# Two heads of a pair in one product at the inverse's second level, Silu on ScalarE, and decay tiles by head

## The chip, the cores and the metric

The kernel runs on one core of a Trainium2 chip, as one program. The metric is the device time of one execution in microseconds. Of three timed runs the median is 2611.71 us (2611.56 to 2614.45). TensorE is called PE in the profile (PEld are its weight loads), VectorE DVE, ScalarE ACT, GpSimd POOL, SyncE SP.

## The reference

A trunk of two layers over 512 tokens of width 1024. Each layer normalises x, projects it once into the inputs of three branches and three groups of gates, and adds the gated branches:

```python
for l in range(DEPTH):
    h = rmsnorm(x, norm_mix[l])
    (dq, dk, dv, dz, db, da, sq, sk, sv, iq, ik, iw, xq, gl) = jnp.split(h @ w_in[l], split_pts, axis=-1)
    o_dn = deltanet_branch(dq, dk, dv, dz, db, da, conv_w[l], a_log[l], dt_bias[l], dn_norm[l])
    o_sa = dsa_branch(sq, sk, sv, iq, ik, iw, positions)
    o_xa = memory_branch(xq, rmsnorm(mem, norm_mem[l]), w_mem_kv[l])
    ...
    x = x + merged @ w_out[l]
    h = rmsnorm(x, norm_ffn[l])
    gt, up = jnp.split(h @ w_ffn_in[l], 2, axis=-1)
    x = x + (jax.nn.silu(gt) * up) @ w_ffn_out[l]
return rmsnorm(x, norm_final)
```

The change is in the DeltaNet branch (8 heads of width 128, a causal convolution of 4 taps and Silu on q, k and v, a gated delta rule):

```python
qkv = jax.nn.silu(causal_conv(jnp.concatenate([q_in, k_in, v_in], axis=-1), conv_w))
q = l2norm(q) * DN_DK ** -0.5; k = l2norm(k)
...
decay = jnp.where(incl, jnp.exp(jnp.where(incl, diff, 0.0)), 0.0)
m = jnp.where(strict, jnp.einsum('bnhid,bnhjd->bnhij', kb, kc) * decay, 0.0)
sol = lax.linalg.triangular_solve(m, rhs, left_side=True, lower=True, unit_diagonal=True)
...
o = rmsnorm(o, dn_norm) * jax.nn.silu(z)
```

## The kernel before, in words

Everything is f32. A weight matrix comes as units of 128 x 1024: SP loads a unit into `wr` (three buffers), ACT rounds it to `wh` (L269, three buffers) and DVE takes the rest `wl` (L270, two buffers). A product with weights is three products of rounded parts, hi x hi, hi x lo, lo x hi (L277 to L279), 24 of them for a unit. Tiles of 128 x 512 come from one pool `P` of 43 slots; PSUM has three banks for weight products (`g`), two for small work (`a`), one `r` and two `o`.

The order of the work is made when the program is built. `Flow` holds a clock and a list of chains (generators). Each step of a weight product moves the clock on, and a chain whose time has come gets to write its next piece; `yield pe, lat` says how much PE time the piece took and how long its result needs. Then the framework's own scheduler puts each engine's instructions in an order, by dependencies and priority. On the chip each engine runs its own list in that order and waits on semaphores.

A layer runs: keys and values of the memory (`mem_kv`), the norm (`norm_chain`, with the sum over partitions at L300 and the spread at L308), the small gates (`misc`), index scores, cross attention, then the DeltaNet stage: four pairs of heads, each with `dn_qk` (k and q of both heads through `conv_silu2`), `dn_z` and `dn_v`, and a chain `dn_chain`. In layer 0 the top-k search runs on DVE beside it. After that come sparse attention, the output projection and the feed-forward (L1027 is its Silu).

`conv_silu2` (L528 to L538) copies the product to `x` and scales it into `y` on ACT, adds three shifted taps on DVE (L535), and takes Tanh of y/2 on ACT (L537); DVE then forms (tanh + 1) * y, which is twice Silu (L586 for k and q, L807 for v, L834 for z). The factor 2 is taken out later, in `hdn`, `hnk` and the small constants under the roots.

`decay_tiles` (L540) makes, for four heads, tiles of decays: one tile per chunk t, with the heads side by side. Each is a product with a mask, then Exp on ACT (L559). `dn_chain` transposes and squares k and q (L596, L603), forms k k^T and k q^T (L638) and multiplies them chunk by chunk with the decays (L641, L643, L647).

`inverse` solves the unit triangular blocks. M of 128 x 128 per chunk and head is cut into blocks of 32, whose inverses come from a forward substitution on DVE (L692, L694) over data that SP carries through DRAM (`dm`, `du`). Level one joins blocks of 32 to 64 (L715, L724). Level two joins 64 to 128: M times the upper inverse goes into `pa` (L734), its lower half is copied to `xz` (L735, L736), and a product with the lower inverse goes into `pb` (L741) and, negated, into `ub`. Each head a of a pair has its own `xt[a]`, `xz[a]` and four products per level; `xt` and `xz` hold zeros in the half that is not used.

Of the kernel before, what the change touches and what calls it, by code (L numbers as in the profile page):

```python
# [21 lines left out]
S = 512  # L22
# [94 lines left out]
def kernel(ctx: ExitStack, tc: tile.TileContext, A: dict, out: bass.AP):  # L117
# [171 lines left out]
    def rms_chain(tiles, n, tok, rs):  # L289
# [4 lines left out]
        for k in range(1, 8):  # L294
            q = ybuf()
            SC.activation(q[:, :n], tiles[k], AF.Square)
            V.tensor_add(acc[:, :n], acc[:, :n], q[:, :n])
            yield 0, 0.6
        for m in range(nt):
            PE.matmul(pt[:, m:m + 1], acc[:, m * 128:m * 128 + 128], ones[:, 0:1], start=m == 0, stop=True,  # L300
                      skip_group_check=True)
# [13 lines left out]
    def norm_chain(tiles, gain, act):  # L315
        rs = small([128, S], "nrs", 1)
        yield from rms_chain(tiles, S, small([128, 4], "ntok", 1), rs)
# [33 lines left out]
    def layer(l, xs, mact):  # L351
# [9 lines left out]
        norm = flow.spawn(norm_chain(xs, nmix[:, l], act))  # L361
# [166 lines left out]
    def conv_silu2(ps, l, idx):  # L528
        y, s = ybuf(), sbuf()
# [7 lines left out]
        SC.activation(s, y, AF.Tanh, scale=0.5)  # L537
        return y, s  # L538

    def decay_tiles(tk, grp):  # L540
        gsl = slice(4 * grp, 4 * grp + 4)
# [5 lines left out]
        def chain():  # L547
            for t in range(4):
                rd = []
                for nm in ("gh", "gl"):  # L550
                    r = sb.tile([128, 4, 128], F32R, name="rd" + nm, tag="rd" + nm, bufs=2)
                    V.tensor_mul(r, mb, tk[nm][:, t, gsl][:, :, None].to_broadcast([128, 4, 128]))
                    rd.append(r)
                yield 0, 2.0
                for w, dst in ((strict_r, dc4[t]), (ones_r, eg4[t])):
# [4 lines left out]
                V.tensor_mul(dc4[t], dc4[t], mb)  # L560
                V.tensor_copy(cd4[:, t], eg4[t][:, :, 127])
# [4 lines left out]
    def dn_qk(l, p, pairs, act, tk):  # L566
# [10 lines left out]
        for a in range(2):  # L577
            h = 2 * p + a
            kq.append([big(F32, (128, 2, 2, 128)) for _ in range(2)])
            for j, (kind, base) in enumerate((("dk", 8), ("dq", 0))):  # L580
                ps = gbank()
                gemm(ps, unit((kind, l, h)), act)
                y, s = conv_silu2(ps, l, base + h)
                for b in range(2):
                    bs = slice(256 * b, 256 * b + 256)
                    V.scalar_tensor_tensor(kq[a][b][:, :, j], s[:, bs].rearrange("p (t i) -> p t i", t=2), 1.0,  # L586
                                           y[:, bs].rearrange("p (t i) -> p t i", t=2),
                                           op0=ALU.add, op1=ALU.mult)
# [25 lines left out]
    def dn_chain(l, p, P, kq, tk):  # L614
# [8 lines left out]
        V.tensor_scalar(x, P.ss, 4.0 * EPS, None, op0=ALU.add)  # L623
        rsqrt_small(x, y, w)
        V.scalar_tensor_tensor(hnk, x, 0.5, y, op0=ALU.mult, op1=ALU.mult)
# [3 lines left out]
        V.tensor_scalar(P.sq, P.sq, 128.0 * EPS, 512.0 * EPS * EPS, op0=ALU.mult, op1=ALU.add)  # L629
        for a in range(2):  # L630
# [3 lines left out]
            for t2 in range(2):  # L634
# [4 lines left out]
                for tt in range(2):  # L639
                    t = 2 * t2 + tt  # L640
                    V.scalar_tensor_tensor(P.mt[a][:, t], pam[:, tt, 0], brk[:, a, t:t + 1], dc4[t][:, h4],  # L641
                                           op0=ALU.mult, op1=ALU.mult)
                    V.tensor_mul(P.at[a][:, t], pam[:, tt, 1], dc4[t][:, h4])  # L643
                yield 0.9, 0.5
            for t in range(4):
                qv = kq[a][t // 2][:, t % 2, 1]
                V.tensor_mul(qv, qv, eg4[t][:, h4])  # L647
# [24 lines left out]
    def inverse(l, p, P):  # L672
# [32 lines left out]
        yield 0, 8.0  # L705
# [3 lines left out]
        for a in range(2):  # L709
            for r in (0, 32):  # L710
                V.transpose(xt[a][r:r + 32, :, r:r + 32], ub[a][r:r + 32, :, r:r + 32])
            V.transpose(tt[64:96, a], ub[a][64:96, :, 64:96])
            for t in range(4):
# [7 lines left out]
        for a in range(2):  # L721
# [4 lines left out]
            for r in (0, 64):  # L726
                SC.activation(ub[a][r:r + 32, :, r + 32:r + 64], pu[r:r + 32, a], AF.Copy, scale=-1.0)
        for a in range(2):
            V.transpose(xt[a][32:64, :, 0:32], ub[a][0:32, :, 32:64])
        yield 1.0, 1.5  # L730
        pa = abank((128, 2, 4, 64))
        for a in range(2):
            for t in range(4):
                PE.matmul(pa[:, a, t], mt[a][:, t], xt[a][:, t], start=True, stop=True)  # L734
        SC.copy(xz[0][64:128, :, 0:64], pa[64:128, 0])  # L735
        V.tensor_copy(xz[1][64:128, :, 0:64], pa[64:128, 1])  # L736
        yield 1.8, 0.8
        pb = abank((128, 2, 4, 64))
        for a in range(2):
            for t in range(4):  # L740
# [513 lines left out]
```

## Time and profile before

| | |
|---|---|
| median of three runs | 2611.71 us |
| the profiled execution | 2612.87 us |
| its span, first to last instruction | 2611.1 us |
| PE busy | 2577.6 us (99%), 13336 matmuls |
| DVE busy | 1648.0 us (63%) |
| ACT busy | 1091.7 us (42%) |

The rows below come from one profiled execution, whose time is a little above the median. PE's busy share counts matmuls whose ends are modelled and overlap, so the cost of one is read from the start of it to the start of the next. Times in the timelines are in us from the start of the span. An f32 product counts as two instructions in the profile and as one in the order.

### The profile page before, as it was taken

Reading aid. Unit: us, or ns where it says so; the run is one execution under the profiler, and the core shown is the slowest. Engines: PE = TensorE matmul, PEld = TensorE weight load, DVE = VectorE, ACT = ScalarE, POOL = GpSimd, SP = SyncE. Lnnn points to the kernel's source line nnn. Section 1 sums busy time; section 2 is a strip of 40 time slices with the busy share of each in tenths; the row PEclk is TensorE's granted clock in tenths of the full one; section 3 lists DMA queues with packets and bytes.
Section 4 is the critical chain, followed back from the end, with each engine's and each line's share of the span. In section 5 each row is a group of like instructions: output and inputs, shape, how many; then the busy total and the mean of one; then the engine's idle time right before and its main releaser. Section 6 shows DMA issues by size and latency. Waiting matters only on the chain.

```text
span 2611.1 us, 35686 instructions
## 1 busy us (share of the span) xinstructions
PE 2577.6 (99%) x13336; PEld 2150.4 (82%) x13336; DVE 1648.0 (63%) x3701; ACT 1091.7 (42%) x2094; POOL 51.6 (2%) x124
## 2 busy tenths in 40 slices
PE   8999999999999999999999999999999999999997
PEld 7888887888888888888898888788888888888886
DVE  7895798764665554434478949887456645544344
ACT  5652545442454343323356426553425543333221
POOL 2000000000000000000000000000000000000000
PEclk9999999999999999999999999999999999999998
DMA  6213322224222332223352142222332123232222
GB/s 223 89 58 120 100 71 71 77 71 138 77 70 73 122 100 97 97 98 113 117 168 73 65 129 91 74 69 76 96 113 73 66 81 129 97 97 97 97 95 75
DMA packets 105724, 250.93 MB, mean 96 GB/s; under 512 B 37888, under 2 KB 38528, under 8 KB 105552
## 3 DMA queue, kind: packets, MB, share of 16 engines
q1 hardware_dynamic: 104656, 247.16, 29.2%
q8 instruction: 105, 1.72, 0.3%
q0 software_dynamic: 896, 1.51, 0.2%
q14 instruction: 67, 0.55, 0.1%
HBM read 236.98 MB, written 11.63 MB: 95 GB/s over the span
## 4 chain that ended last, share of the span: by engine, by line
PE 90%; DVE 7%; ACT 2%; issue 1%; DMA 1%; SPq 0%; DVEq 0%; ACTq 0%
PE g L277 26%; PE g L278 26%; PE g L279 26%; DVE y L535 2%; DVE wl L270 1%; PE o L277 1%; PE a L638 1%; PE a L279 1%; PE a L277 1%; PE a L278 1%; PE r L960 1%; PE o L278 1%; DVE utmp L692 1%; PE o L279 1%; DVE u L694 1%
## 5 line engine op out<-in xcount | busy, mean ns | idle before, releaser
L270 DVE TENSOR_TENSOR wl<-wr,wh 128x1024 fp32r<-128x1024 f32 (+1 forms) x418 | 506.3, 1211 | 570.1 <-PE g L279 397.0
L277 PE MATMUL g<-hh,wh 128*128 128x512 f32 (+1 forms) x2064 | 821.6, 398 | 0.0
L278 PE MATMUL g<-hl,wh 128*128 128x512 f32 (+1 forms) x2064 | 814.0, 395 | 0.0
L279 PE MATMUL g<-hh,wl 128*128 128x512 f32 (+1 forms) x2064 | 812.7, 394 | 0.0
L269 ACT CAST wh<-wr 128x1024 fp32r<-128x1024 f32 (+1 forms) x418 | 436.7, 1045 | 840.0 <-PE g L278 689.2
L279 PEld LDWEIGHTS g<-hh,wl 128*128 128x128 f32 (+1 forms) x2064 | 387.8, 188 | 77.0
L278 PEld LDWEIGHTS g<-hl,wh 128*128 128x128 f32 (+1 forms) x2064 | 388.7, 188 | 70.9 <-DVE hl L167 0.5
L277 PEld LDWEIGHTS g<-hh,wh 128*128 128x128 f32 (+1 forms) x2064 | 388.5, 188 | 70.7
L277 PE MATMUL g<-P,wh 128*128 128x512 f32 (+1 forms) x992 | 374.1, 377 | 7.4 <-ACT wh L269 7.4
L279 PE MATMUL g<-P,wl 128*128 128x512 f32 (+1 forms) x992 | 373.7, 377 | 0.5 <-DVE wl L270 0.5
L278 PE MATMUL g<-P,wh 128*128 128x512 f32 (+1 forms) x992 | 373.6, 377 | 0.0
L277 PEld LDWEIGHTS g<-P,wh 128*128 128x128 f32 x992 | 188.0, 190 | 41.2 <-ACT wh L269 7.5
L279 PEld LDWEIGHTS g<-P,wl 128*128 128x128 f32 x992 | 187.9, 189 | 34.6 <-DVE wl L270 0.8
L278 PEld LDWEIGHTS g<-P,wh 128*128 128x128 f32 x992 | 188.0, 190 | 33.5
L535 DVE SCALAR_TENSOR_TENSOR y<-x,k_conv_w,y 128x511 f32<-128x511 f32 x144 | 107.5, 746 | 7.9 <-ACT y L532 6.7
L167 DVE TENSOR_TENSOR P<-y,P 128x512 fp32r<-128x512 f32 (+1 forms) x86 | 59.4, 690 | 46.3 <-ACT P L166 46.3
L166 ACT CAST P<-y 128x512 fp32r<-128x512 f32 (+1 forms) x86 | 53.4, 620 | 83.1 <-DVE y L1031 43.8
L278 PE MATMUL g<-wl,hh 128*128 128x256 f32 x256 | 72.4, 283 | 0.0
L279 PE MATMUL g<-wh,hl 128*128 128x256 f32 x256 | 72.4, 283 | 0.0
L277 PE MATMUL g<-wh,hh 128*128 128x256 f32 x256 | 72.4, 283 | 0.0
L166 ACT CAST P<-r 128x256 fp32r<-128x256 f32 (+2 forms) x96 | 39.0, 406 | 64.1 <-PE r L960 45.4
L537 ACT ACTIVATE s<-y 128x512 f32<-128x512 f32 x48 | 30.3, 632 | 81.1 <-DVE y L535 70.0
(295 smaller groups left out, 3179.6 us busy)
## 6 DMA issues: line engine op xcount, KB each, us to landing
wr<-wu SPq DMA_DIRECT2D x400, 512.0 KB, 3.5
wr<-wf SPq DMA_DIRECT2D x16, 384.0 KB, 3.1
P<-xT SPq DMA_DIRECT2D x16, 256.0 KB, 5.1
park<-P SPq DMA_DIRECT2D x16, 256.0 KB, 4.1
P<-dm SPq DMA_DIRECT2D x64, 64.0 KB, 2.0
P<-park SPq DMA_DIRECT2D x16, 256.0 KB, 4.5
P<-memT SPq DMA_DIRECT2D x8, 256.0 KB, 4.6
d_x<-P SPq DMA_DIRECT2D x8, 256.0 KB, 4.1
```

Source lines behind the costliest of these rows:

```text
L166: SC.copy(hi, src)
L167: V.tensor_sub(lo, src, hi)
L269: SC.copy(wh[:, :cols], raw[:, :cols])
L270: V.tensor_sub(wl[:, :cols], raw[:, :cols], wh[:, :cols])
L277: PE.matmul(ps, lh, rh, start=start, stop=False, skip_group_check=skip)
L278: PE.matmul(ps, lh, rl, start=False, stop=False, skip_group_check=skip)
L279: PE.matmul(ps, ll, rh, start=False, stop=stop, skip_group_check=skip)
L535: V.scalar_tensor_tensor(y[:, sh:], x[:, :S - sh], cw[:, l, idx, j:j + 1], y[:, sh:], op0=ALU.mult, op1=ALU.add)
L537: SC.activation(s, y, AF.Tanh, scale=0.5)
L638: PE.matmul(pam[:, tt], kk[:, 0], kk, start=True, stop=True)
L692: V.tensor_mul(tv, u[:, :n, j:j + 1].to_broadcast([128, n, m]), mp[j // 16][:, j % 16:j % 16 + 1, j + 1:].to_broadcast([128, n, m]))
L694: V.tensor_sub(u[:, :n, j + 1:], u[:, :n, j + 1:], tv)
```

## The change

Level two of the inverse now treats both heads of a pair in one product. A new buffer `mz` takes the block of M that is needed, head 0's in rows 0 to 63 and columns 64 to 127, head 1's in rows 64 to 127 and columns 0 to 63, by two DMAs on SP's queue. Level one puts head 1's `xt` into the lower half of `xt[0]` with a copy on ACT, and head 1's lower inverse into the upper right of `ub[0]` with another, and `pa` and `pb` are four products each for the pair. Since `mz`, `xz` and `xt[0]` are shared, a list `packing` lets one pair at a time into this part; the waiting times in the yields change with it (8 to 7 and at least one more, 1.5 to 2.0, 1.8 to 0.9).

`conv` no longer takes Tanh; ACT applies Silu to y and writes k and q (two halves each) or v in place, and z straight from PSUM. The factors of 2 go: `4 * EPS` becomes `EPS`, the 0.5 in `hnk` and `hdn` falls away. Decay tiles are made per head with the four chunks side by side, so that DVE multiplies two chunks at once (L643 and L647 of before). The norm of layer 0 gets 4 units of waiting ahead of its sum over partitions.

```diff
...
-    def norm_chain(tiles, gain, act):
+    def norm_chain(tiles, gain, act, wait=0.0):
...
+        yield 0, wait
...
-        norm = flow.spawn(norm_chain(xs, nmix[:, l], act))
+        norm = flow.spawn(norm_chain(xs, nmix[:, l], act, 0.0 if l else 4.0))
...
-    def conv_silu2(ps, l, idx):
-        y, s = ybuf(), sbuf()
+    def conv(ps, l, idx):
+        y = ybuf()
...
-        SC.activation(s, y, AF.Tanh, scale=0.5)
-        return y, s
+        return y
...
-            for t in range(4):
+            for h in range(4):
                 rd = []
                 for nm in ("gh", "gl"):
                     r = sb.tile([128, 4, 128], F32R, name="rd" + nm, tag="rd" + nm, bufs=2)
-                    V.tensor_mul(r, mb, tk[nm][:, t, gsl][:, :, None].to_broadcast([128, 4, 128]))
+                    V.tensor_mul(r, mb, tk[nm][:, :, 4 * grp + h:4 * grp + h + 1].to_broadcast([128, 4, 128]))
                     rd.append(r)
                 yield 0, 2.0
-                for w, dst in ((strict_r, dc4[t]), (ones_r, eg4[t])):
+                for w, dst in ((strict_r, dc4[h]), (ones_r, eg4[h])):
                     pd = abank((128, 4, 128))
                     PE.matmul(pd, w, rd[0], start=True, stop=False)
                     PE.matmul(pd, w, rd[1], start=False, stop=True)
                     SC.activation(dst, pd, AF.Exp)
-                V.tensor_mul(dc4[t], dc4[t], mb)
-                V.tensor_copy(cd4[:, t], eg4[t][:, :, 127])
+                V.tensor_mul(dc4[h], dc4[h], mb)
+                V.tensor_copy(cd4[:, :, h], eg4[h][:, :, 127])
...
-                y, s = conv_silu2(ps, l, base + h)
+                y = conv(ps, l, base + h)
                 for b in range(2):
                     bs = slice(256 * b, 256 * b + 256)
-                    V.scalar_tensor_tensor(kq[a][b][:, :, j], s[:, bs].rearrange("p (t i) -> p t i", t=2), 1.0,
-                                           y[:, bs].rearrange("p (t i) -> p t i", t=2),
-                                           op0=ALU.add, op1=ALU.mult)
+                    SC.activation(kq[a][b][:, :, j], y[:, bs].rearrange("p (t i) -> p t i", t=2), AF.Silu)
...
-                for tt in range(2):
-                    t = 2 * t2 + tt
-                    V.scalar_tensor_tensor(P.mt[a][:, t], pam[:, tt, 0], brk[:, a, t:t + 1], dc4[t][:, h4],
+                for t in (2 * t2, 2 * t2 + 1):
+                    V.scalar_tensor_tensor(P.mt[a][:, t], pam[:, t % 2, 0], brk[:, a, t:t + 1], dc4[h4][:, t],
                                            op0=ALU.mult, op1=ALU.mult)
-                    V.tensor_mul(P.at[a][:, t], pam[:, tt, 1], dc4[t][:, h4])
+                ts = slice(2 * t2, 2 * t2 + 2)
+                V.tensor_mul(P.at[a][:, ts], pam[:, :, 1], dc4[h4][:, ts])
                 yield 0.9, 0.5
-            for t in range(4):
-                qv = kq[a][t // 2][:, t % 2, 1]
-                V.tensor_mul(qv, qv, eg4[t][:, h4])
+            for t2 in range(2):
+                qv = kq[a][t2][:, :, 1]
+                V.tensor_mul(qv, qv, eg4[h4][:, 2 * t2:2 * t2 + 2])
...
-        yield 0, 8.0
+        yield 0, 7.0
+        while packing:
+            yield 0, 1.0
+        packing.append(p)
+        SP.dma_start(mz[0:64, :, 64:128], mt[0][0:64, :, 64:128])
+        SP.dma_start(mz[64:128, :, 0:64], mt[1][0:64, :, 64:128])
+        yield 0, 1.0
...
+            if a:
+                SC.copy(xt[0][64:128], xt[1])
...
+        SC.copy(ub[0][0:64, :, 64:128], ub[1][64:128, :, 64:128])
         for a in range(2):
-            V.transpose(xt[a][32:64, :, 0:32], ub[a][0:32, :, 32:64])
-        yield 1.0, 1.5
-        pa = abank((128, 2, 4, 64))
-        for a in range(2):
-            for t in range(4):
-                PE.matmul(pa[:, a, t], mt[a][:, t], xt[a][:, t], start=True, stop=True)
-        SC.copy(xz[0][64:128, :, 0:64], pa[64:128, 0])
-        V.tensor_copy(xz[1][64:128, :, 0:64], pa[64:128, 1])
-        yield 1.8, 0.8
-        pb = abank((128, 2, 4, 64))
-        for a in range(2):
-            for t in range(4):
-                PE.matmul(pb[:, a, t], xz[a][:, t], ub[a][:, t, 64:128], start=True, stop=True)
-        SC.activation(ub[0][0:64, :, 64:128], pb[0:64, 0], AF.Copy, scale=-1.0)
-        V.tensor_scalar(ub[1][0:64, :, 64:128], pb[0:64, 1], -1.0, None, op0=ALU.mult)
-        yield 1.8, 0.8
+            V.transpose(xt[0][64 * a + 32:64 * a + 64, :, 0:32], ub[a][0:32, :, 32:64])
+        yield 1.0, 2.0
+        pa = abank((128, 4, 64))
+        for t in range(4):
+            PE.matmul(pa[:, t], mz[:, t], xt[0][:, t], start=True, stop=True)
+        SC.copy(xz[64:128, :, 0:64], pa[64:128])
+        V.tensor_copy(xz[0:64, :, 64:128], pa[0:64])
+        yield 0.9, 0.8
+        pb = abank((128, 4, 64))
+        for t in range(4):
+            PE.matmul(pb[:, t], xz[:, t], ub[0][:, t, 64:128], start=True, stop=True)
+        SC.activation(ub[0][0:64, :, 64:128], pb[0:64], AF.Copy, scale=-1.0)
+        V.tensor_scalar(ub[1][0:64, :, 64:128], pb[64:128], -1.0, None, op0=ALU.mult)
+        packing.clear()
+        yield 0.9, 0.8
...
-            y, s = conv_silu2(ps, l, 16 + h)
-            V.scalar_tensor_tensor(y, s, 1.0, y, op0=ALU.add, op1=ALU.mult)
+            y = conv(ps, l, 16 + h)
+            SC.activation(y, y, AF.Silu)
...
-            s = sbuf()
-            SC.activation(s, ps, AF.Tanh, scale=0.5)
             z = big()
-            V.scalar_tensor_tensor(z, s, 1.0, ps, op0=ALU.add, op1=ALU.mult)
+            SC.activation(z, ps, AF.Silu)
...
-    xt = [cst([128, 4, 64], name=f"xt{a}") for a in range(2)]
-    xz = [cst([128, 4, 128], name=f"xz{a}") for a in range(2)]
-    for t_ in xt + xz:
+    xt = [cst([128, 4, 64], name="xt0"), cst([64, 4, 64], name="xt1")]
+    xz, mz = (cst([128, 4, 128], name=n) for n in ("xz", "mz"))
+    packing = []
+    for t_ in xt + [xz, mz]:
...
```

Three places in the order show how instructions move. The first is PE in the second pair of layer 0, around level two: `xt_76` and `xt_77` are the two heads' tiles, `mz` the new buffer, `g` rows are weight products. Before:

```order
L278 MATMUL g<-hl,wh 128x512
L734 MATMUL a<-xt_76,P 128x64 x4
L734 MATMUL a<-xt_77,P 128x64 x4
L279 MATMUL g<-hh,wl 128x512
L277 MATMUL g<-hh,wh 128x512
L278 MATMUL g<-hl,wh 128x512
L741 MATMUL a<-P,xz_78 128x64 x4
L741 MATMUL a<-P,xz_79 128x64 x4
L596 MATMUL a<-k_ident,P 128x128 x4
```

And now:

```order
L278 MATMUL g<-hl,wh 128x512
L739 MATMUL a<-xt_76,mz 128x64 x4
L279 MATMUL g<-hh,wl 128x512
L277 MATMUL g<-hh,wh 128x512
L278 MATMUL g<-hl,wh 128x512
L279 MATMUL g<-hh,wl 128x512
L277 MATMUL g<-hh,wh 128x512
L745 MATMUL a<-P,xz 128x64 x4
L593 MATMUL a<-k_ident,P 128x128 x4
```

Eight products each have become four, and five weight products stand between them in place of three. Over the program PE has 12488 products before and 12424 now.

The second place is ACT at the first head of layer 0's DeltaNet stage, where convolution, activation and the decay tiles' Exp (L559, now L558) meet. Before:

```order
L269 CAST wh<-wr 128x1024
L531 COPY x<-g 128x512
L532 ACTIVATE y<-g,k_conv_w 128x512
L537 ACTIVATE s<-y 128x512
L559 ACTIVATE P<-a 128x512 x2
```

And now:

```order
L269 CAST wh<-wr 128x1024
L532 COPY x<-g 128x512
L533 ACTIVATE y<-g,k_conv_w 128x512
L585 ACT_TABLE_LOAD
L585 ACTIVATE P<-y 128x2x128 x2
L558 ACT_TABLE_LOAD
L558 ACTIVATE P<-a 128x512 x2
```

A table load stands ahead of Silu and another ahead of Exp. The program has 6 table loads before and 26 now. On PE the first transposes of k (L596, now L593) stand eleven weight products further back.

The third place is DVE at the start, around the norm's last square sums (L297) and the reading of L300's result (L303, now L304). Before:

```order
L297 TENSOR_TENSOR s<-s,y 128x512 x2
L270 TENSOR_TENSOR wl<-wr,wh 128x1024
L297 TENSOR_TENSOR s<-s,y 128x512
L847 TENSOR_TENSOR y<-g,mrs 128x512
L303 TENSOR_SCALAR rx<-a 128x4
L270 TENSOR_TENSOR wl<-wr,wh 128x1024
L608 TENSOR_SCALAR ntok<-rx 128x4
```

And now:

```order
L297 TENSOR_TENSOR s<-s,y 128x512 x2
L270 TENSOR_TENSOR wl<-wr,wh 128x1024
L297 TENSOR_TENSOR s<-s,y 128x512
L850 TENSOR_TENSOR y<-g,mrs 128x512
L270 TENSOR_TENSOR wl<-wr,wh 128x1024
L167 TENSOR_TENSOR P<-y,P 128x512
L304 TENSOR_SCALAR rx<-a 128x4
L605 TENSOR_SCALAR ntok<-rx 128x4
```

A weight's low half and another subtraction have moved ahead of the reading of the sum. On PE, L300 (now L301) stands eighteen weight products further back.

## Rows read from the trace of the kernel before

**Rows 1.** The page's head and its first two parts: the span, TensorE's busy time, share and instructions, and the clock that was granted in 40 slices (tenths of the full level).

```profile
span 2611.1 us, 35686 instructions
...
PE 2577.6 (99%) x13336; PEld 2150.4 (82%) x13336; DVE 1648.0 (63%) x3701; ACT 1091.7 (42%) x2094; POOL 51.6 (2%) x124
...
PEclk9999999999999999999999999999999999999998
```

**Rows 2.** The page's fourth part: shares of the chain of waits that ended last, by engine.

```profile
PE 90%; DVE 7%; ACT 2%; issue 1%; DMA 1%; SPq 0%; DVEq 0%; ACTq 0%
```

**Rows 3.** The list of PE's waits over the whole span: who waited, line and engine that ended it, us in total, number of waits, longest.

```profile
PE g L278 <- DVE wl L270: 2.1, 2, 1.2
PE r L763 <- DVE S L779: 1.1, 1, 1.1
PE a L638 <- DVE utmp L692: 1.0, 1, 1.0
PE a L638 <- DVE u L694: 1.0, 1, 1.0
PE a L638 <- DVE P L643: 0.8, 2, 0.4
PE a L715 <- DVE xt L711: 0.6, 1, 0.6
PE a L755 <- ACT P L742: 0.5, 1, 0.5
PE g L279 <- DVE wl L270: 0.5, 1, 0.5
PE r L666 <- ACT P L796: 0.4, 2, 0.2
PE r L666 <- DVE P L793: 0.4, 2, 0.2
```

**Rows 4.** The groups of PE by line, the second level's two products: forms, count, busy us, mean ns of one, idle before.

```profile
L734 PE MATMUL a<-xt,P 128*128 128x64 f32 x128 | 16.1, 272 | 0.0
L741 PE MATMUL a<-P,xz 128*128 128x64 f32 x128 | 15.4, 271 | 0.0
```

**Rows 5.** The timeline of PE in layer 0's second pair, around the products into `pa`: start us, us, line, operation, output and operands, forms, number merged.

```profile
419.30 0.40 PE L278 MATMUL g<-hl,wh 128*128 128x512 f32 x1
419.53 1.89 PE L734 MATMUL a<-xt,P 128*128 128x64 f32 x16
421.23 0.47 PE L279 MATMUL g<-hh,wl 128*128 128x512 f32 x1
421.55 0.39 PE L277 MATMUL g<-hh,wh 128*128 128x512 f32 x1
```

**Rows 6.** The timeline of PE at the start, around the norm's sum over partitions (L300), with the idle time ahead of a row and what ended it in brackets.

```profile
45.42 0.28 PE L277 MATMUL g<-wh,P 128*128 128x256 f32 x1
...
45.66 0.28 PE L279 MATMUL g<-wh,P 128*128 128x256 f32 x1
48.23 1.87 PE L300 MATMUL a<-ones,s 128*128 128x1 f32 x8 [2.29 <-DVE s L297]
```

**Rows 7.** Three stretches of the first 100 us: start and end, us, busy us and instructions of PE, PEld, DVE, ACT and POOL, then the granted clock, DMA share and GB/s.

```profile
41.00:47.80 6.80, 3.70 (x29) 3.29 (x28) 4.97 (x7) 3.90 (x7) 2.15 (x5) 1.00 1.04 357
47.80:54.60 6.80, 6.37 (x30) 6.37 (x31) 4.06 (x13) 2.67 (x3) 0.53 (x1) 0.51 0.55 176
...
92.20:95.60 3.40, 3.40 (x10) 2.62 (x9) 1.92 (x3) 2.61 (x4) 0.00 (x0) 0.51 0.00 0
```

**Rows 8.** The timeline of DVE in the same place: the low half of a weight and the last square sum.

```profile
46.35 1.22 DVE L270 TENSOR_TENSOR wl<-wr,wh 128x1024 fp32r<-128x1024 f32 x1
47.49 0.69 DVE L297 TENSOR_TENSOR s<-s,y 128x512 f32<-128x512 f32 x1
```

**Rows 9.** The stretch of layer 0's DeltaNet stage, same columns as in Rows 7.

```profile
270.00:600.00 330.00, 326.81 (x1922) 267.59 (x1922) 259.91 (x805) 163.18 (x442) 3.15 (x6) 1.00 0.25 78
```

**Rows 10.** The timeline of ACT in layer 1's small gates: an activation, a table load and the next activation.

```profile
1365.98 0.23 ACT L451 ACTIVATE t_beta<-tok 128x32 f32<-128x32 f32 x1
1366.23 1.28 ACT L455 ACT_TABLE_LOAD   x1
1367.52 0.23 ACT L455 ACTIVATE t_e<-t_e 128x32 f32<-128x32 f32 x1
```

**Rows 11.** Groups of ACT by line and form: count, busy us, mean ns of one, idle before and what ended it.

```profile
L537 ACT ACTIVATE s<-y 128x512 f32<-128x512 f32 x48 | 30.3, 632 | 81.1 <-DVE y L535 70.0 <-DVE utmp L692 8.6 <-DVE ow L611 1.8
...
L1027 ACT ACTIVATE y<-s 128x512 f32<-128x512 f32 x44 | 27.8, 632 | 41.4 <-DVE s L1026 41.4
...
L166 ACT CAST P<-r 128x256 fp32r<-128x256 f32 x48 | 17.9, 372 | 21.4 <-PE r L898 11.6 <-DVE P L167 6.6 <-PE r L960 2.7
...
L735 ACT COPY xz<-a 64x256 f32<-64x256 f32 x8 | 2.9, 368 | 10.6 <-PE a L734 10.5
```

**Rows 12.** The timeline of ACT in the first pair of layer 0, where Tanh waited for the convolution.

```profile
278.08 0.63 ACT L537 ACTIVATE s<-y 128x512 f32<-128x512 f32 x1 [2.93 <-DVE y L535]
```

**Rows 13.** Groups of DVE by line and form: the two combinations of Tanh's result with its argument.

```profile
L586 DVE SCALAR_TENSOR_TENSOR P<-s,y 128x256 f32<-128x256 f32 x64 | 25.9, 420 | 5.4 <-ACT s L537 5.2
...
L807 DVE SCALAR_TENSOR_TENSOR y<-s,y 128x512 f32<-128x512 f32 x16 | 11.0, 689 | 2.4 <-ACT s L537 2.2
```

**Rows 14.** The page's sixth part, DMA issues: count, KB each, median us from issue to landing.

```profile
P<-dm SPq DMA_DIRECT2D x64, 64.0 KB, 2.0
```

More of the change, by code (lines that the diff above doesn't have):

```diff
@@ L287, in gemm, with rms_chain @@
             flow.tick(tick)
-    def rms_chain(tiles, n, tok, rs):
+    def rms_chain(tiles, n, tok, rs, wait=0.0):
         nt = n // 128
@@ L313, in rms_chain @@
         return ps
-    def norm_chain(tiles, gain, act):
+    def norm_chain(tiles, gain, act, wait=0.0):
         rs = small([128, S], "nrs", 1)
-        yield from rms_chain(tiles, S, small([128, 4], "ntok", 1), rs)
+        yield from rms_chain(tiles, S, small([128, 4], "ntok", 1), rs, wait)
         for k in range(8):
@@ L536, in conv_silu2 @@
                                    op0=ALU.mult, op1=ALU.add)
-        SC.activation(s, y, AF.Tanh, scale=0.5)
-        return y, s
+        return y
     def decay_tiles(tk, grp):
-        gsl = slice(4 * grp, 4 * grp + 4)
         eg4 = [big(F32, (128, 4, 128)) for _ in range(4)]
@@ L622, in dn_chain @@
         hnk = small([128, 2, 4], "hnk", 3)
-        V.tensor_scalar(x, P.ss, 4.0 * EPS, None, op0=ALU.add)
+        V.tensor_scalar(x, P.ss, EPS, None, op0=ALU.add)
         rsqrt_small(x, y, w)
-        V.scalar_tensor_tensor(hnk, x, 0.5, y, op0=ALU.mult, op1=ALU.mult)
+        V.tensor_mul(hnk, x, y)
         V.tensor_mul(w, y, y)
@@ L628, in dn_chain @@
         P.hnk = hnk
-        V.tensor_scalar(P.sq, P.sq, 128.0 * EPS, 512.0 * EPS * EPS, op0=ALU.mult, op1=ALU.add)
+        V.tensor_scalar(P.sq, P.sq, 128.0 * EPS, 128.0 * EPS * EPS, op0=ALU.mult, op1=ALU.add)
         for a in range(2):
@@ L1102, in start @@
         V.tensor_scalar(hbg, hbg, 0.5, None, op0=ALU.mult)
-        V.tensor_scalar(hdn, hdn, 0.5, None, op0=ALU.mult)
         SC.activation(ealog, ealog, AF.Exp)
```

## The prediction

> **What bounds the kernel now.** I read the page first: TensorE is busy for 2577.6 of 2611.1 us and its clock is at the full level in all slices but the last [rows 1]. The chain of work that ended last puts 90% of the span on PE and only 7% on DVE and 2% on ACT [rows 2]. The list of PE's waits then says where PE stood still: almost nothing. Outside the start and the two final norms, the DeltaNet stages hold eight small rows, from "L763" to "L666", which add up to 1.1 + 1.0 + 1.0 + 0.8 + 0.6 + 0.5 + 0.4 + 0.4 = 5.8 us over both layers [rows 3]. So a microsecond of PE work taken out is a microsecond of time, as long as no wait comes in, and work taken from DVE buys nothing by itself: the windows put DVE at 259.91 and ACT at 163.18 of 330 us in the first DeltaNet stage [rows 9].
>
> **The change part by part, first PE.** The second level of the inverse was 8 products into `pa` and 8 into `pb` for each pair of heads; now it is 4 and 4. The profile counts two instructions for each f32 product: 128 for L734 and 128 for L741 over eight pairs [rows 4], so 64 + 64 = 128 go. Their mean of 272 and 271 ns is no price, since neighbours overlap. The price is read from starts: sixteen of L734 begin at 419.53 and the next L279 at 421.23, so 1.70 us; that L279 holds the engine for 0.32 us (421.23 to 421.55) where L278 before the piece held it for 0.23 (419.30 to 419.53), so 0.09 more belong to the piece [rows 5]. That makes 1.79 / 16 = 0.112 us each, or 0.106 without the tail. 128 x 0.112 = **14.3 us** go (13.6 by the lower price). No wait of note stands before these pieces, so this time lies on the path.
>
> **The pieces of small work.** Counted in the order, PE's stream of weight products is broken 408 times before and 425 times now. A break costs between nothing (the last instruction of a piece is shorter by what the next product is longer) and that 0.09 us [rows 5]: 17 breaks give 0 to +1.5 us. I take **+0.5**, nearer the lower end, because the eight-pair sum above already carries the tail.
>
> **The start.** Layer 0's norm now waits 4 units of the planner before its sum over partitions (L300). Before, PE stood 2.29 us until DVE had the last square sum, at 48.23 [rows 6], while the next weights' low half was ready before that: it ran 46.35 to 47.57, the last sum 47.49 to 48.18 [rows 8]. Right behind that, the granted clock was 0.51 from 47.8 to 54.6 us, the lower of the two levels (1.2 GHz), after PE had been busy for only 3.70 of 6.80 us [rows 7]; at half speed for 6.8 us, about 3.3 us of work were lost. The order now has eighteen products more ahead of L300, at 0.12 us each (45.42 to 45.66 holds two) [rows 6]: 2.2 us to lay into the wait. Part of them need that low half, so PE stands until 47.57 in place of 48.23 with part of the work done: 1.2 us less. The best case is the whole 2.29 us and the whole 3.3 us of the low clock, -5.6. The worst is that the norm's chain (sums, scale, eight normalised tiles) lands later by those 2.2 us and PE waits for it at the first projection, +2.2. I take **-2.5**: the 1.2 us and somewhat under half of the 3.3, because a shorter gap may or may not keep the clock up.
>
> **ScalarE and VectorE.** DVE loses 64 combinations of 420 ns and 16 + 16 of 689 and about as much, some 49 us in all [rows 13], and half of the small products with the decay tiles. ACT computes 64 activations fewer of the old kind and as many Silus; the same form of Silu in the feed-forward took 632 ns as Tanh did, so the function costs the same. The q and k ones are cut in two: 2 x 0.37 (the 128x256 cast) - 0.63 = +0.1 us, 32 times. Sixteen copies of 64 partitions at 368 ns are new, 5.9 us [rows 11]. And the order shows twenty more table loads, because Exp of the decay tiles and Silu don't share a table: 20 x 1.28 = 25.7 us on ACT [rows 10]. All that is about 35 us on an engine which idles half of these stages. What hides the loads: the load stands ahead of Silu, and ACT used to idle 2.93 us there until the convolution came [rows 12]; the one back to Exp has no such gap ahead, but the order also moved the transposes that need Silu's result some eleven products, 2.5 us, further back. If that cover is gone, every load costs up to 1.28 us of PE time; the rival below takes it all. On the other side the eight waits of 5.8 us are mostly for DVE, which now has less to do. Between -5.8 and +5.9 (the sixteen copies laid bare; the loads apart) I take **0** for new and old waits together.
>
> The Trainium skill (ScalarE: Activation LUTs, "What ACT_TABLE_LOAD costs") speaks against the change: it says that a switch of table costs its load of about 1283 ns and a drain of about 1380 ns, 2.66 us together. By it the loads would hold ACT for 53 us, an estimate from that page. The trace agrees with the load and shows no drain: the Tanh at 1365.98 ends at 1366.21, the load runs 1366.23 to 1367.51, the Exp starts at 1367.52 [rows 10]. So I count the load alone.
>
> **The two DMAs of each pair** that copy blocks of M into `mz` go into SP's queue behind the loads of `dm`, and behind them stand weight loads. 64 KB took 2.0 us to land [rows 14]; the data they need are there when `dm` starts, and the product that reads `mz` comes a whole forward substitution later. The second pair's copies wait until the first pair's product has read `mz`; weights for two units are already issued ahead of that. I cost them at nothing; if a weight load slips behind one it is 2.0 us, sixteen at most, and I hold none of them for likely.
>
> **Sum.** -14.3 + 0.5 - 2.5 + 0 = -16.3 us. The profiled execution took 2612.87 us (span 2611.1 and 1.8 around it), so 2596.6 by itself; it lies 1.2 us above the median of 2611.71, and from the median I get **2595.5 us**.
>
> **Rivals.**
> - *The serial steps eat it.* Level two now runs one chain per pair in place of two that overlap; two copies, the shared buffers and ACT's queue (a weight cast of a microsecond may stand ahead) lie in it. Eight pairs with about 1 us of new wait each are +8: about 2603.5. For it: the sums `pa` of one head used to cover the copy of the other. Against: the order sets five products, 1.1 us, between `pa` and `pb` of the second pair, against 368 ns for the copy [rows 11].
> - *Table loads on PE's path: slower.* Place: the decay stage of pairs 0 and 2 in both layers, where Exp, Silu and Exp alternate on ACT. Price 1.28 us each, twenty of them: -14.3 + 25.7 = +11.4, about 2623. It decides from the eleventh exposed load on (11 x 1.28 = 14.1). For it: the loads are certain. Against: PE had no wait for Exp or Tanh in these stages [rows 3], and the idle ACT has ahead of the activation is longer than a load. By the price of the Trainium skill above it would be decided from the sixth load on, an estimate (6 x 2.66 = 16); no row here bears that out.
> - *More comes loose.* The 5.8 us of waits, the 2.29 and the 3.3 us of the first low clock and the 1.7 us of the second (0.51 from 92.2 to 95.6 us [rows 7]) all go: -14.3 - 5.8 - 5.6 - 1.7 = -27.4, about 2584.
> - *It doesn't do what it says*: the products halve in number, but PE waits for weights in their place (DVE's low halves, DMA). Then nothing changes: 2607 to 2612. Against: PE's waits for a low half come to 2.1 and 0.5 us in the whole span [rows 3].
>
> **How the numbers follow.** The forecast has 0.70, with its own range 2590 to 2601; the serial steps 0.12, more loose 0.08, no gain 0.06, slower 0.04. The range of 8 in 10 takes in the unknown terms (-5.6 to +2.2 at the start, -5.8 to +5.9 in the stages, which do not all fall to one side): 2587 to 2604. A measurement of this kernel tells about 0.2%, 5.2 us, from no change. Faster by more: the forecast, the looser case and nearly all of the serial one, 0.88. Within: 0.08, no gain and the rest of the serial one. Slower: 0.04.
>
> **What would show it.** Right: the rows of the second level's products are half as many (64 and 64) at the same 0.112 us from start to start; PE's waits in the DeltaNet stages stay near 5.8 us; the wait ahead of L300 is shorter; 26 table loads of 1.28 us stand on ACT and no PE wait names Silu or Exp. Wrong: rows of PE waiting for `xz`, `xt`, Silu's tiles or a weight behind `mz`; a longer stretch at 0.5 of the clock; a new wait for the normalised tiles at the first projection.

## The result, and the profile after

The changed kernel took 2597.1 us (median of 6 executions, 2594.0 to 2598.7) against 2612.0 us before: a ratio of 0.9942, with a 95% interval of 0.9933 to 0.9952, so 15.1 us less (12.5 to 17.5). The forecast was 2595.5 us, with a range of 2587 to 2604. The profiled execution took 2596.0 us.

The page's head, TensorE's clock and the shares of the chain, to be laid beside [rows 1, 2]:

```profile
span 2594.2 us, 35329 instructions
...
PE 2564.1 (99%) x13208; PEld 2132.6 (82%) x13208; DVE 1608.6 (62%) x3540; ACT 1126.9 (43%) x2162; POOL 52.0 (2%) x124
...
PEclk9999999999999999999999999999999999999999
...
PE 91%; DVE 5%; ACT 1%; DMA 1%; issue 1%; SPq 0%; DVEq 0%; ACTq 0%
```

PE lost the 128 instructions (13336 to 13208) and 13.5 us of busy time. DVE lost 39.4 us and ACT gained 35.2, and neither moved the end: PE bounds the kernel as before.

The list of PE's waits (us in total, times, longest), for [rows 3]:

```profile
PE a L720 <- DVE xt L714: 0.8, 2, 0.5
PE a L473 <- DVE t_g L468: 0.6, 1, 0.6
PE a L635 <- DVE u L691: 0.5, 1, 0.5
...
PE a L635 <- DVE utmp L689: 0.5, 1, 0.5
...
PE a L739 <- issue: 0.2, 1, 0.2
```

L473 lies in the gates. The DeltaNet stages keep 0.8 + 0.5 + 0.5 + 0.2 = 2.0 us of waits, where they had 5.8. One row names `xt` (0.8 us); the kernel before had one of 0.6, and both are level one's. None names Silu, Exp, `xz` or a weight behind `mz`.

The groups of level two's products, for [rows 4], and ACT's new table loads (count, busy us, mean ns, idle before):

```profile
L739 PE MATMUL a<-xt,mz 128*128 128x64 f32 x64 | 8.5, 275 | 0.4 <-issue 0.2
...
L745 PE MATMUL a<-P,xz 128*128 128x64 f32 x64 | 8.1, 270 | 0.0
```

```profile
L585 ACT ACT_TABLE_LOAD x10 | 12.8, 1283 | 11.9 <-DVE y L536 8.4 <-issue 2.6 <-DVE ow L608 0.9
...
L558 ACT ACT_TABLE_LOAD x8 | 10.3, 1283 | 0.1
```

Half as many products at the same mean. Measured from each one's start to the next start, level two took 27.8 us before and 13.6 now: -14.2. Eighteen of the loads stand at Silu (L585) and Exp (L558); with two at L954 they are the twenty new ones.

Five stretches, same columns as [rows 7, 9]:

```profile
18.00:22.00 4.00, 3.50 (x16) 3.50 (x17) 3.72 (x21) 0.22 (x1) 0.00 (x0) 0.57 0.49 154
41.00:47.80 6.80, 5.30 (x44) 5.10 (x43) 4.75 (x8) 4.77 (x7) 2.35 (x5) 1.00 1.03 334
47.80:54.60 6.80, 6.60 (x54) 6.19 (x52) 6.09 (x15) 3.89 (x6) 1.15 (x3) 1.00 0.79 287
92.20:95.60 3.40, 3.40 (x16) 2.81 (x15) 3.27 (x6) 1.78 (x4) 0.00 (x0) 1.00 0.39 154
270.00:600.00 330.00, 327.92 (x1882) 264.14 (x1881) 239.69 (x724) 179.52 (x474) 3.15 (x6) 1.00 0.29 87
```

Both stretches of [rows 7] that ran at 0.51 now run at 1.00, the full level. But this profile has a low stretch of its own at 18 to 22 us, where the one before read 1.00. The wait ahead of the norm's sum over partitions is gone in the timeline of PE (compare [rows 6]), while one of 0.88 us has come ahead of the spread (L309), where that profile had none:

```profile
49.76 0.28 PE L279 MATMUL g<-wh,P 128*128 128x256 f32 x1
49.88 0.95 PE L301 MATMUL a<-ones,s 128*128 128x1 f32 x8
...
55.40 1.16 PE L309 MATMUL a<-k_ident,ntok 128*128 128x128 f32 x8 [0.88 <-DVE ntok L609]
```

Setting the start of the same weight product beside the same one before shows where the time went: the changed kernel is 3.8 us ahead when the start is over (119 us), 5.4 us more after layer 0's DeltaNet stage, 7.4 us more after layer 1's; between the stages next to nothing moves.

### The profile page after: what moved, and what is told of

Same layout as the page of the kernel before. It is cut to its first block, busy times and chain, and to the rows that moved or that the text cites. A ratio compares the mean times of both kernels' runs of the same rounds, so it can differ in the third digit from the quotient of the medians.

```text
span 2594.2 us, 35329 instructions
## 1 busy us (share of the span) xinstructions
PE 2564.1 (99%) x13208; PEld 2132.6 (82%) x13208; DVE 1608.6 (62%) x3540; ACT 1126.9 (43%) x2162; POOL 52.0 (2%) x124
## 4 chain that ended last, share of the span: by engine, by line
PE 91%; DVE 5%; ACT 1%; DMA 1%; issue 1%; SPq 0%; DVEq 0%; ACTq 0%
PE g L277 26%; PE g L279 26%; PE g L278 26%; PE a L635 1%; DVE wl L270 1%; PE o L277 1%; DVE utmp L689 1%; DVE u L691 1%; PE o L278 1%; PE r L963 1%; PE o L279 1%; DVE y L536 1%; PE a L279 1%; PE a L277 1%; PE a L278 1%
## 5 line engine op out<-in xcount | busy, mean ns | idle before, releaser
L536 DVE SCALAR_TENSOR_TENSOR y<-x,k_conv_w,y 128x511 f32<-128x511 f32 (+1 forms) x144 | 106.7, 745 | 7.6 <-ACT y L533 6.5
L167 DVE TENSOR_TENSOR P<-r,P 128x256 fp32r<-128x256 f32 (+2 forms) x96 | 44.4, 462 | 26.0 <-ACT P L166 25.4
```

The costliest lines, as they stand in the source:

```text
L167: V.tensor_sub(lo, src, hi)
L536: V.scalar_tensor_tensor(y[:, sh:], x[:, :S - sh], cw[:, l, idx, j:j + 1], y[:, sh:], op0=ALU.mult, op1=ALU.add)
```

## The experiments

Each time is a median over five rounds, each ratio is to the kernel before on the same chip, with its 95% interval.

**One part alone.** Four kernels hold one part of the change each. A line or two stand for each part here, and where a part is taken away below; the rest of the edit is that part of the diff above:

```diff
# e1_pack_only: level two as in the change
-                PE.matmul(pa[:, a, t], mt[a][:, t], xt[a][:, t], start=True, stop=True)
+            PE.matmul(pa[:, t], mz[:, t], xt[0][:, t], start=True, stop=True)
# e2_silu_only
-        SC.activation(s, y, AF.Tanh, scale=0.5)
+                    SC.activation(kq[a][b][:, :, j], y[:, bs].rearrange("p (t i) -> p t i", t=2), AF.Silu)
# e3_decay_only
-                for w, dst in ((strict_r, dc4[t]), (ones_r, eg4[t])):
+                for w, dst in ((strict_r, dc4[h]), (ones_r, eg4[h])):
# e4_wait_only
-        norm = flow.spawn(norm_chain(xs, nmix[:, l], act))
+        norm = flow.spawn(norm_chain(xs, nmix[:, l], act, 0.0 if l else 4.0))
```

> Only the second level's packing is made (with its buffers, DMAs and copies); Tanh, decay tiles by chunk and the start stay as before. Theory (PE's time goes one for one): 128 PE instructions at 0.112 us are gone, 14.3 us, so a ratio of about 0.9945 (2597.5 to 2600), and about 7 us of it in each layer's DeltaNet stage. Rival (the gain of the whole change came from the work taken off DVE and from the start, and the serial steps of the packed level ate the products' gain): within 5 us of before, 2607 or more.

Measured: 2606.1 us, 0.9977 (0.9968 to 0.9987). That lies between the two theories' ranges, close to the rival's: far less gain than the products that go.

> Only Silu on ScalarE in place of Tanh and the combination on DVE, with about twenty more table loads. Theory (loads hidden, DVE no bound): no change, within 3 us of 2612. Rival (loads lie on PE's path): slower by several us, up to 11 after the DVE relief, 2616 to 2625. Second rival (DVE relief is what pays): faster by 4 us or more.

Measured: 2609.9 us, 0.9993 (0.9985 to 1.0002): as the first theory said. Its profile has 28 table loads, and they do no harm.

> Only decay tiles by head, so that DVE multiplies two chunks in one instruction. Theory: no change, within 2 us of 2612, since PE waits 5.8 us in both stages together and only part of that is for these products. Rival (DVE relief pays): faster by 3 us or more.

Measured: 2615.1 us, 1.0014 (1.0005 to 1.0023): a little slower, which neither theory had.

> Only the 4 units of waiting ahead of the norm's sum in layer 0. Theory: faster by 2 to 4 us (2608 to 2610), all of it before 110 us of the span, and the stretch of the lower clock near 48 us shorter or gone. Rival (the start's gain in the changed kernel came by chance of the clock, not by the wait): no change, and the clock still falls near 48 us.

Measured: 2610.2 us, 0.9991 (0.9983 to 1.0000), at the edge of the first theory's range; its profile has neither low stretch of [rows 7].

By these ratios the four parts add up to -6.0 - 1.8 + 3.7 - 2.4 = -6.5 us; together they gave -15.1. The profile of e1 shows one reason. The timelines of PE and then of DVE in layer 0's third pair, brackets holding the idle time ahead:

```profile
491.57 0.51 PE L279 MATMUL g<-hh,wl 128*128 128x512 f32 x1
492.94 1.07 PE L742 MATMUL a<-xt,mz 128*128 128x64 f32 x8 [0.86 <-ACT c L603]
494.92 1.10 PE L748 MATMUL a<-P,xz 128*128 128x64 f32 x8 [0.91 <-DVE xz L744]
495.86 0.80 PE L596 MATMUL a<-k_ident,P 128*128 128x128 f32 x4
```

```profile
491.16 1.30 DVE L758 TENSOR_TENSOR P<-P,t_eg 128x512 f32<-128x512 f32 x2
492.49 0.30 DVE L738 STREAM_TRANSPOSE xt<-P 32x128 f32<-32x128 f32 x1
...
494.45 0.42 DVE L744 COPY xz<-a 64x256 f32<-64x256 f32 x1 [0.34 <-ACT xz L743]
```

PE's wait is put down to a square on ACT (L603), which ended at 492.80. At the same time, 492.79, the transpose ended that makes `xt`, which had stood behind 1.30 us of two large elementwise products on DVE; then the copy of `xz` came after the whole of the first four products, and nothing lay between the halves. What it cost shows in the windows (columns as in [rows 7]):

```profile
492.00:494.00 2.00, 1.14 (x9) 0.97 (x8) 1.94 (x4) 1.79 (x9) 0.00 (x0) 1.00 0.00 0
494.00:496.00 2.00, 1.09 (x11) 1.08 (x11) 1.67 (x5) 1.92 (x4) 0.00 (x0) 1.00 0.04 8
496.00:498.00 2.00, 2.00 (x9) 1.71 (x8) 1.81 (x5) 1.84 (x10) 0.00 (x0) 0.54 0.19 45
498.00:500.00 2.00, 2.00 (x11) 1.81 (x11) 0.89 (x5) 0.37 (x1) 0.00 (x0) 0.61 0.55 217
```

PE was busy for 2.23 of 4 us, and the granted clock then fell to about the lower level (1.2 GHz) for most of the next 4. The seventh pair repeats it (waits of 0.5 and 0.9 us, then 0.60 from 1780 to 1788 us). The changed kernel at the same step of the same pair, in its timeline of PE:

```profile
482.21 1.08 PE L739 MATMUL a<-xt,mz 128*128 128x64 f32 x8
483.09 0.48 PE L278 MATMUL g<-hl,wh 128*128 128x512 f32 x1
...
485.25 0.39 PE L278 MATMUL g<-hl,wh 128*128 128x512 f32 x1
485.48 1.07 PE L745 MATMUL a<-P,xz 128*128 128x64 f32 x8
```

Ten weight products lie between the halves, there is no wait, and the clock stays. e3 has the same in the same pair: the order left one weight product ahead of the second half, PE waited 1.7 us, and two of its windows read:

```profile
496.00:498.00 2.00, 0.69 (x6) 0.69 (x7) 1.94 (x3) 2.00 (x11) 0.00 (x0) 1.00 0.01 2
498.00:500.00 2.00, 2.00 (x12) 2.00 (x11) 1.29 (x3) 0.32 (x1) 0.00 (x0) 0.50 0.71 260
```

**The gap filled.** e5 is e1 with a longer pause after the first half:

```diff
# e5_pack_fill, against e1_pack_only
-        yield 0.9, 0.8
+        yield 0.9, 2.0
```

> The packed level two alone, as in e1_pack_only, with one number changed: the pause after its first four products is 2.0 instead of 0.8, so that the order puts weight products of the next units between the first and the second four in every pair (5, 3 to 5 of them, where e1_pack_only had none in the third and the seventh pair). Theory 'empty gap': what e1_pack_only lost is the TensorE idle time of 1.4 to 1.8 us in these two pairs and the half clock that followed it (3.4 and 6.8 us at half level, so 1.7 and 3.4 us), about 8 us where both come. Without the gap no wait for xz or c of over 0.3 us, granted clock 1.00 from 470 to 520 us and from 1770 to 1800 us, time 2598 to 2600.5 us. Rival 'the parts need each other' (the pack gains only with less VectorE work, from Silu): the time stays at 2605 to 2607 us, waits of the same size at other lines.

Measured: 2604.2 us, 0.9968 (0.9955 to 0.9980). A miss for both theories. The waits for `xz` went and layer 0's stage kept the full clock: 323.4 us, between the same weight products, against 327.8 in e1. But in layer 1 a gap came back one step earlier, at level one: the list of waits has `L723 <- DVE c L718` with 1.8 us, and the windows around it are

```profile
1762.00:1772.00 10.00, 8.20 (x51) 6.25 (x49) 4.39 (x8) 3.67 (x5) 0.00 (x0) 1.00 0.42 118
1772.00:1780.00 8.00, 8.00 (x74) 5.97 (x75) 5.19 (x10) 4.66 (x17) 0.00 (x0) 0.79 0.11 40
```

So the gap belongs to the order, not to level two as such: a small shift decides which step goes bare.

**One part taken away from the whole.** Four kernels are the changed one without one part:

```diff
# e6_tanh_back
-        return y
+        SC.activation(s, y, AF.Tanh, scale=0.5)
+        return y, s
# e7_no_pack
-            PE.matmul(pa[:, t], mz[:, t], xt[0][:, t], start=True, stop=True)
+                PE.matmul(pa[:, a, t], mt[a][:, t], xt[a][:, t], start=True, stop=True)
# e8_no_decay
-                for w, dst in ((strict_r, dc4[h]), (ones_r, eg4[h])):
+                for w, dst in ((strict_r, dc4[t]), (ones_r, eg4[t])):
# e9_no_wait
-        norm = flow.spawn(norm_chain(xs, nmix[:, l], act, 0.0 if l else 4.0))
+        norm = flow.spawn(norm_chain(xs, nmix[:, l], act))
```

> The changed kernel with the tanh form of Silu put back (scale 0.5 on ScalarE, the product on VectorE, and its constants), the packed level two, the decay tiles by head and the pause in the start kept. In its order every pair has 5 or more weight products between the two halves of level two, but for one with 2. Theory 'empty gap': the Silu matters for its own small gain only (e2_silu_only: 1.5 us), since the gap is covered without it: 2598 to 2601 us, no half clock after 120 us but perhaps at the pair with 2 products near 1780 us. Rival 'less VectorE work makes the pack work': 2603 to 2607 us, with waits for the xz copies and a half clock in both layers' stages.

Measured: 2600.1 us, 0.9954 (0.9941 to 0.9966).

> The changed kernel with the level two of before (16 products for each of two steps and pair), the Silu, the decay tiles by head and the pause in the start kept. Theory of the prediction (the product term is the change): 2608 to 2611.5 us, so 11.5 to 14.5 us more than the changed kernel, and no wait of before comes back. Rival 'sum of the parts as each measured alone' (pack worth 5.4 us): 2602 to 2603.5 us.

Measured: 2608.3 us, 0.9989 (0.9980 to 0.9998).

> The changed kernel with the decay tiles by token block as before, all else kept. In its order every pair has 5 or more weight products between the halves of level two. Theory 'empty gap': what e3_decay_only lost (3.6 us) was the wait of 1.7 us and the half clock of 6.8 us at the one place where only one weight product stood between the halves; that place is covered in the changed kernel, so the decay tiles are worth 0 there: 2596 to 2598.5 us. Rival 'decay by head costs by itself' (more work ahead of the first products): 2592.5 to 2594.5 us, faster than the changed kernel.

Measured: 2596.3 us, 0.9940 (0.9927 to 0.9954).

> The changed kernel without the pause of 4 units in the first layer's norm; all else kept. Theory of the prediction (the start term, put at 2.5 us): the wait for s at the norm's first product (2.3 us) and the half clock that followed it in the profile of before (about 8 us at half level from 48 to 56 us) come back, so the time rises by 2 to 4.5 us over the changed kernel's 2597.1: 2599 to 2601.5 us. Rival 'as measured alone' (the pause alone gave 1.3 us): 2597.5 to 2598.9 us.

Measured: 2599.4 us, 0.9950 (0.9937 to 0.9962). The wait and the dip are back, in its timeline of PE and in its window:

```profile
49.76 1.37 PE L300 MATMUL a<-ones,s 128*128 128x1 f32 x8 [2.93 <-DVE s L297]
```

```profile
47.80:54.60 6.80, 4.84 (x25) 4.84 (x26) 4.73 (x10) 2.71 (x3) 1.07 (x3) 0.69 0.50 188
```

The dip doesn't hang on the pause alone, though. The profile of e7, which has the pause and no wait ahead of L301, shows it too:

```profile
47.80:54.60 6.80, 5.45 (x28) 5.45 (x29) 5.68 (x13) 3.12 (x4) 0.69 (x2) 0.65 0.69 252
```

All four fall where the first theory of each put them:

| part | alone, us | in the whole, us |
|---|---|---|
| packed level two | -6.0 | -12.3 |
| Silu | -1.8 | -3.1 |
| pause in the start | -2.4 | -2.1 |
| decay tiles by head | +3.7 | +0.5 |
| sum (whole change: -15.1) | -6.5 | -17.0 |

Each number is a difference of ratios times 2611.7 us, and the interval of each ratio alone is 2 to 3.5 us to either side. Within the whole, the packing is most of the gain and the parts nearly add up; alone they don't, because two of them open gaps that the others' order covers. Of the small rows, the intervals of e6 and e9 overlap with that of the changed kernel, and the decay tiles can't be told from nothing.

**The pause ahead of the inverse.** e10 was made to put a gap back, e11 and e12 to explain its result:

```diff
# e10_late_pause (e12_later_pause: 20.0), against the changed kernel
-        yield 0, 7.0
+        yield 0, 14.0
# e11_before_late, against the kernel before
-        yield 0, 8.0
+        yield 0, 15.0
```

> The changed kernel with the pause ahead of the inverse's first products 14 instead of 7, nothing else. In its order the second, third, sixth and seventh pair then have no or one weight product (and one or two other products) ahead of the first four products of level two, where the changed kernel has 3 to 8; the instructions are the same ones in the same numbers. Theory 'empty gap': TensorE idles about 1 us in each of these four pairs, and the granted clock falls to its lower level behind at least one of them: 2601 to 2609 us, mean clock of the two DeltaNet stages under 1.00, waits for the copies of level one or two. Rival 'the work left out is what counts' (gaps cost nothing that is not made good elsewhere): 2596 to 2598.5 us.

Measured: **2587.0 us**, 0.9905 (0.9890 to 0.9921). Both theories missed: it is 10 us faster than the changed kernel. The two DeltaNet stages of the profiled executions took 319.3 + 339.9 us against 324.9 + 343.9, -9.6 us. Counting weight products ahead of a step was the wrong measure: with the pause, what the step reads was ready. And level one's first step changed its shape. In the changed kernel its 32 small instructions of a pair stand in four pieces; two of them, in PE's timeline of the seventh pair, are

```profile
1749.72 0.39 PE L277 MATMUL g<-hh,wh 128*128 128x512 f32 x1
1750.05 0.24 PE L720 MATMUL a<-xt,P 32*32 32x32 f32 x2
1750.22 0.50 PE L278 MATMUL g<-hl,wh 128*128 128x512 f32 x1
1750.56 0.40 PE L279 MATMUL g<-hh,wl 128*128 128x512 f32 x1
...
1751.25 0.50 PE L277 MATMUL g<-hh,wh 128*128 128x512 f32 x1
```

and in e10 the eighth pair's stand in one:

```profile
1811.53 0.39 PE L279 MATMUL g<-hh,wl 128*128 128x512 f32 x1
1811.85 0.21 PE L720 MATMUL a<-xt,P 32*32 32x32 f32 x1
...
1812.47 0.50 PE L277 MATMUL g<-hh,wh 128*128 128x512 f32 x1
```

Weight products alone follow each other by 0.23 us. The two pieces add (1750.22 - 1749.72 - 0.23) + (1751.25 - 1750.56 - 0.23) = 0.27 + 0.46 = 0.73 us for half of a pair, so 1.46 for a pair in four pieces; the single piece adds 1812.47 - 1811.53 - 0.23 = 0.71. So **a break by these 32 x 32 products costs about 0.25 us**, besides the 0.11 us by which the weight product behind it is longer (1750.22 to 1750.56, against 0.23). In the whole trace this step's pieces went from 32 to 16 and their time by the same reckoning from 13.1 to 8.2 us: half of the 9.6 us. The other half is spread over many kinds and stays unassigned. Breaks as such aren't what counts: in the traces, PE's stream of weight products is broken 424 times in the changed kernel and 429 times in e10.

> The kernel before with one number changed: the pause ahead of the inverse's first products 15 instead of 8, so that it is late by as much as e10_late_pause is. In its order the small products of level one's first step stand in 19 pieces between other work instead of 30 (in e10_late_pause 16, in the changed kernel 32). Theory 'pieces and transposes': e10_late_pause gained because these products no longer wait for VectorE's transposes one by one, which has nothing to do with the packing; here 13 pieces fewer of the 16 there give 4 to 8 us: 2603 to 2607.5 us. Rival 'the pause pays only together with the packing' (it spreads the turns of the pairs at the shared tiles): 2610 to 2613 us.

Measured: 2606.5 us, 0.9980 (0.9971 to 0.9989), in the first theory's range: the pause pays without the packing too. Less, though, 5.2 us against 9.7. Eleven pieces of level one's first step fewer (19 for 30) at 0.25 + 0.11 make 4.0 of it, an estimate, and the listed waits of the stages fell by 1.6 (5.8 to 4.2). The breaks of the whole stream rose here too, from 407 to 434.

> The changed kernel with the pause 20 instead of 7 (e10_late_pause has 14). In its order level one's first step stands in 9 pieces (32 in the changed kernel, 16 in e10_late_pause), and every pair has 6 or more weight products between the halves of level two. Theory 'pieces and transposes': 3 to 5 us less than e10_late_pause's 2587.0: 2582 to 2585 us. Rival 'a later inverse delays what waits for it' (the heads' steps come late, the third and fourth pair's end too): 2588 to 2596 us.

Measured: 2589.5 us, 0.9912 (0.9899 to 0.9926). Nine pieces and no further gain: the stages took 320.2 + 340.5 us, a little more than in e10. The time lies in the rival's range. Fewer pieces of this one step aren't the whole of it, then; past 14 something gives back what they save, and no run here says whether it is the rival's delay.

## Why the prediction was right

- **The products** (-14.3): right, -14.2 from start to start, and e7 shows that the packing carries most of the change, -12.3 us with what it does to the order.
- **The pieces** (+0.5): small, as forecast, though a little over its bound of 1.5, since breaks don't all cost the same. Ahead of a full product nothing is added (485.25 to 485.48, 0.23 us). In the trace of the kernel before, eight of level two's instructions in one piece add 0.82 us (median of nine pieces) and sixteen 1.71 (of seven), and either way the weight product behind is longer by 0.09. So one break more among full products costs 2 x 0.91 - 1.80 = 0.02, while one by 32 x 32 products costs 0.25 + 0.11. Of the 17 more breaks four are of the dear kind (50 pieces hold such products, 46 before). An estimate from these figures is 4 x 0.36 + 13 x 0.02 = +1.7.
- **Waits new and old** (0, bounds -5.8 to +5.9): mis-sized. The listed ones fell from 5.8 to 2.0 us, -3.8, with DVE busy for 39.4 us less. Products, pieces and waits together make -14.2 + 1.7 - 3.8 = -16.3, against -5.4 - 7.4 = -12.8 seen in the stages. So 3.5 us were lost in places that the list of waits doesn't show, and their cause is open. Stalls too short for that list may be part of it: the pieces of eight instructions of level two add 0.89 us in the changed kernel (median of twelve), 0.82 in e10 (of ten). The prediction took 0 for all waits together; that a gain of 3.8 and a loss of 3.5 nearly cancelled is luck.
- **The start** (-2.5): the size came out, the working less so. e9 gives back 2.1 by the ratios, e4 gave 2.4 alone, each with an interval at least as wide. The 2.29 us of wait at the sum went whole, and not by 1.2; but 0.88 us came back at the spread, a delay of the norm's chain such as the worst case held. The clock's part is not settled: low stretches at the start come and go from profile to profile, in e7 with the pause, in the changed kernel at 18 to 22 us. So the 3.8 us between the two profiles are not the worth of the pause.
- **The table loads** (hidden, -0 to +25.7): right. ACT's timeline in layer 0 shows why:

```profile
274.22 1.28 ACT L585 ACT_TABLE_LOAD   x1 [2.91 <-DVE y L536]
275.51 0.73 ACT L585 ACTIVATE P<-y 128x256 f32<-128x256 f32 x2
276.25 1.28 ACT L558 ACT_TABLE_LOAD   x1
277.55 1.09 ACT L558 ACTIVATE P<-a 128x512 f32<-128x512 f32 x2
```

  ACT is idle 2.91 us ahead of the first, PE has no wait behind the second. The next activation starts 0.01 to 0.02 us after a load, and the second load 0.01 us after the activation ahead. The drain of about 1380 ns per switch, which the Trainium skill (ScalarE: Activation LUTs, "What ACT_TABLE_LOAD costs") adds, isn't there in this order either.
- **The DMAs into `mz`** (nothing): right, no wait on `mz` is listed.
- **The rivals.** *The serial steps eat it* is the one that came near: level two's chain does go bare, by 0.9 us for `xz` as feared, in e1, though not in the changed kernel, where ten products cover it. What the rival left out is the clock that falls behind such a gap. Of *more comes loose*, part was seen: 3.8 us of the waits, and, in the profiled execution, both low stretches of the start, against a new one. The table loads on PE's path and the change that does nothing were not seen.

That single parts would not add up was nowhere in the prediction. For e1, products (-14.2), waits (6.9 in place of 5.8) and the low clock of pairs three and seven (1.7 + 3.4 us lost, from the windows) make -8.0, while its stages fell by 3.9: some 4 us there are open.

## What to carry to other kernels

Where a planner sets the order, price a change also by what it breaks the bounding engine's stream with: a break by small 32 x 32 products cost about 0.25 us here and 0.11 more on the product behind, one by full products next to nothing. Test a part by taking it out of the finished kernel rather than by putting it alone into the old one, since an order that has no cover left at one step can hide most of a part's worth. And try the planner's pauses again after such a change: one number took off 10 us more, 2587.0 us against 2597.1.

## What the runs showed of the hardware

The clock fell behind gaps shorter than the 2.29 us of [rows 6]. After 4 us with PE busy for 2.23 (e1) the granted clock was 0.54 for 2 us, after 2 us with 0.69 busy (e3) it was 0.50, and after 10 us with 8.20 (e5) it was 0.79 over the next 8. The single waits of 1.0 and 1.1 us in layer 0's stage of the kernel before [rows 3] left it at 1.00 [rows 9]. That the clock follows how busy TensorE has been is also what the Trainium skill says (TensorE: Matmul & The Clock Gate, "What's actually happening"). In e1 the twelve executions differ by it: five with a mean granted clock of 0.994 took 2606.0 to 2610.1 us, the two with 0.998 took 2600.2 and 2600.7, just above the 2597.5 to 2600 us that the first theory gave the part.
